# Two-layer hybrid decoder trunk on one core: later readers behind queued transposes, TensorE transposes half a step later, interleaved first loads, Strassen products for two gate projections

## The chip, the core and the metric

The kernel runs on one core of one Trainium2 chip. The metric is the device time of one execution in microseconds (us), lower is better. TensorE does the matrix products, VectorE (DVE in the profile) and ScalarE (ACT) prepare operands and finish results, GpSimd (POOL) and SyncE (SP) issue transfers; each engine works through its own queue in program order.

## The reference, cut to what matters

Two layers, 256 tokens, model width 2048, everything in float32.

```python
for l in range(DEPTH):                                   # 2
    h = rms_norm(x, mix_norm[l])
    proj = h @ w_in[l]                                   # 2048 -> q 1024 | k 256 | v 256 | u,v 2048 | gates 4096
    q, k, v, uv, gate_logits = jnp.split(proj, cuts, axis=-1)
    ...
    branch_a = sliding_window_attention(q, k, v, sinks[l]) @ w_attn_branch[l]       # 1024 -> 2048
    branch_b = chunked_sgu(jax.nn.gelu(uv), w_spatial[l], ...) @ w_sgu_branch[l]    # 1024 -> 2048
    gates = jax.nn.sigmoid(gate_logits)
    merged = gates[..., :D_MODEL] * branch_a + gates[..., D_MODEL:] * branch_b
    x = x + merged @ w_out[l]
    h2 = rms_norm(x, ffn_norm[l])
    x = x + (jax.nn.silu(h2 @ w_gate[l]) * (h2 @ w_up[l])) @ w_down[l]              # 2048 -> 5632 -> 2048
return x
```

## The kernel before

**A product in three passes.** A float32 product is made of three matmuls (`three`, L318): high part by high part, high by low, low by high. For the weights, ScalarE rounds a loaded piece to its high part (`whi`, L222) and VectorE subtracts it to get the low part (`wlo`, L230), always 128x1024 at a time, for a matrix that is used once. For the activations, a "unit" of 512 rows of the contraction holds `uh` and `ul` (transposed high and low part, L426 and L433, or L451 and L438), for all 256 tokens.

**Jobs and steps.** The work is a list of jobs (`add_job`, L106), each one 1024 (or 512) output columns of one weight matrix, run one after the other by `run` (L323). A plain job goes over its units; each unit gives four steps of 12 matmuls (two halves of the rows, two halves `c` of the columns). A step is one slot of time in the schedule (`tick`, L269). In the order of a layer the jobs are: q and k/v, v, u, gate a (columns 0 and 1024), branch a (0, 1024), then gate b 0, branch b 0, gate b 1024, branch b 1024, then w_out 0 and 1024, then three feed-forward rounds of gate, up and down jobs (blocks 0 to 3, 4 to 7, and 8 to 10). The names used below are gate-b-0, gate-b-1024 and so on; "up job of blocks 2 and 3" is the up projection of those two 512-column blocks.

**Strassen jobs.** With `m=1` (L43: w_out, gate/up and down) the first unit of a job is done by a seven-product scheme in place of eight: products 11, t1, t2, 22, t3, 21, t4 (L87) of 6 matmuls each, half a slot each. It needs sums of weight pieces (`sum` and `raw`, L214, four VectorE operations of 128x1024) and sums of activation blocks (`sums`, `sh`, `sl`, L450 to L458). Between the products, results move among PSUM banks: ScalarE copies `a` into `x` after 11 (L358), `e` into `p` after t1 and `a` into `u` after t2 (L344), `a` into `y` after t3 (L364); VectorE adds `u` and `p` back after t4 (L366, L367). Product 22 overwrites `e`, so it waits for `p`; t3 overwrites `a`, so it waits for `u`; t4 waits for `y`; the plain step that accumulates into `e` waits for L366.

**Transposes.** A new activation is transposed in one of two ways (`transposed`, L416). Gathered: VectorE transposes 32x32 blocks (`blk`, L408), then GpSimd issues 16 small transfers (`tt<-blk`, L413), and a fixed `G_WAIT` = 5 slots later ScalarE reads `tt` into `uh`, a slot later VectorE makes `ul`. On TensorE (`on_pe`, L471): eight 128x128 transposes into PSUM (`pt`), from which ScalarE makes `uh` at once and VectorE `ul` a slot later. The third block of each product's output goes through TensorE, the others are gathered.

**What sets the order.** Each engine's order is written by hand. `after(n, f)` puts work n slots later, `soon` behind the operand preparation of the next step; `fill` (L234) keeps high parts six and low parts five pieces ahead of TensorE. Results of a job's two column halves come out in its last two steps: `scaled_into`, `gated` (L948, with `merge` L960 in branch b), `upped` (L994) or the residual add (L895), all on VectorE, and two `Square` passes per block on ScalarE (`junk`, L513).

Of the kernel before, what the change touches and what calls it, by code (L numbers as in the profile page):

```python
# [14 lines left out]
P = 128  # L15
NT = 2
S = P * NT
# [31 lines left out]
def hybrid_trunk(ctx: ExitStack, tc: tile.TileContext, x, mix_norm, w_in, q_norm, k_norm, sinks,  # L49
# [84 lines left out]
    for l in range(DEPTH):  # L134
        wl = w_in[l]
        for o in (0, None)[::-1 if l == 0 else 1]:
            add_job([wl[:, o:o + CW2] if o is not None else wl[:, O_KV:O_KV + CW]])
        for o in (O_V, O_U, O_GATE, O_GATE + CW2):
            add_job([wl[:, o:o + CW2]])
        for o in (0, CW2):  # L140
            add_job([w_attn_branch[l, :, o:o + CW2]])
        for o in (0, CW2):
            add_job([wl[:, O_GATE + D + o:O_GATE + D + o + CW2]])
            add_job([w_sgu_branch[l, :, o:o + CW2]])
# [114 lines left out]
    def after(n, fn):  # L259
        steps.append((slot_no[0] + n, fn))  # L260
# [123 lines left out]
    class Unit:  # L384


        def __init__(self, sums):
            self.hi = slot([P, 4, S], F32R, "uh")
            self.lo = slot([P, 4, S], F32R, "ul")
            if sums:  # L390
                self.shi = slot([P, 4, 2, P], F32R, "sh")
                self.slo = slot([P, 4, 2, P], F32R, "sl")

        def block(self, name, k):
            if name in ("11", "21", "t4"):
# [4 lines left out]

    def flat(v):
        return v.rearrange("p a b -> p (a b)") if len(v.shape) == 3 else v.rearrange("p a b c -> p (a b c)")

    def gathered(dst, src):

        blk = slot([P, 4, 4, NT, B], name="blk")
        for t in range(NT):
            nc.vector.transpose(blk[:, :, :, t, :].rearrange("p j k c -> p k j c"),  # L408
                                src[:, t, :].rearrange("p (k j c) -> p k j c", j=4, c=B))
        ov = dst.rearrange("p k (t i c) -> p i (k t) c", t=NT, c=B)  # L410
        for i in range(4):
            for j in range(4):
                nc.gpsimd.dma_start(ov[j * B:(j + 1) * B, i],  # L413
                                  blk[i * B:(i + 1) * B, j].rearrange("p k t c -> p (k t) c"))

    def transposed(units, c, src, scale=None, cols=None, on_pe=False, sums=False, at_once=False):  # L416

        unit = Unit(sums)

        def scaled(k):  # L420
            return (scale or 1.0) if cols is None else cols[:, k:k + 1]

        def highs(k0, n, src_t):
            step = n if cols is None else 1
            for k in range(0, n, step):
                nc.scalar.activation(unit.hi[:, k0 + k:k0 + k + step, :], src_t[:, k:k + step, :], AF.Copy,  # L426
                                     scale=scaled(k0 + k))
# [9 lines left out]
        def low(hi, lo, full):  # L437
            nc.vector.tensor_tensor(out=flat(lo), in0=flat(full), in1=flat(hi.bitcast(F32)), op=ALU.subtract)  # L438

        def ready():  # L440
            units[c] = unit

        def combined(f, n):
            s4 = slot([P, 4, 2, P], name="sums")
            a11, a12, a21, a22 = (f[:, 2 * h:2 * h + 2, t * P:(t + 1) * P] for t in range(2) for h in range(2))

            def first():
                for i, (p, q, op) in enumerate(((a21, a22, ALU.add), (s4[:, 0], a11, ALU.subtract),
                                                (a11, a21, ALU.subtract), (a12, s4[:, 1], ALU.subtract))):
                    nc.vector.tensor_tensor(out=s4[:, i], in0=p, in1=q, op=op)  # L450
                nc.scalar.activation(unit.hi, f, AF.Copy)  # L451

            def second():
                low(unit.hi, unit.lo, f)
                nc.scalar.activation(unit.shi, s4, AF.Copy)

            def third():
                low(unit.shi, unit.slo, s4)  # L458
                ready()

            for i, fn in enumerate((first, second, third)):
                after(n + i, fn)

        if on_pe:
            pts = []
            for b in range(2):
                pt = ps_at.tile([P, 2, S], F32, tag="at", name=nm("pt"))
                for kk in range(2):
                    k = 2 * b + kk
                    for t in range(NT):  # L470
                        nc.tensor.transpose(pt[:, kk, t * P:(t + 1) * P], src[:, t, k * P:(k + 1) * P], ident)  # L471
# [12 lines left out]
            return  # L484

        tt = slot([P, 4, S], name="tt")
        gathered(tt, src)
        if not sums:
            after(G_WAIT, lambda: highs(0, 4, tt))
            after(G_WAIT + 1, lambda: (lows(0, 2, tt[:, 0:2]), lows(2, 2, tt[:, 2:4]), ready()))  # L490
            return

        def scale_all():
            if cols is not None or scale is not None:
                for k in range(4) if cols is not None else (None,):
                    kk = slice(0, 4) if k is None else slice(k, k + 1)
                    nc.scalar.activation(tt[:, kk], tt[:, kk], AF.Copy, scale=scaled(k))

        after(G_WAIT, scale_all)
        combined(tt, G_WAIT + 1)  # L500

    class Norm:


        def __init__(self, cols):
            self.cols = cols
            self.ss = [tiny(NCH, f"ss{t}", 2) for t in range(NT)]
            self.units = [None] * NCH

        def squares(self, c):  # L510
            for t in range(NT):
# [139 lines left out]
    class Attention:  # L651
# [62 lines left out]
        def begin(self):  # L714
            n = Q_FIRST
            for c in range(2):
                for t in range(NT):
                    for g in (2 * c, 2 * c + 1):
                        after(n, lambda t=t, g=g: self.scores(t, g))
                        n += Q_STEP  # L720
                after(n + 7, lambda c=c: transposed(self.attT, c, self.att[c]))

        def scores(self, t, g):
            nk = P * (t + 1)
# [64 lines left out]
    class Spatial:  # L789
# [61 lines left out]
        def u(self, c, ps):  # L851
            ut = slot([P, NT, CW], name="u")
            self.gelu(ps, ut)
            for b in range(2):
                after(12 + 3 * b + 6 * c, lambda b=b: self.mix(c, b, ut))
            after(19 + 6 * c, lambda: transposed(self.sguT, c, ut))

        def mix(self, c, b, ut):
            pg = ps_at.tile([P, 2, NT, P], F32, tag="at", name=nm("psg"))
# [44 lines left out]
    for l in range(DEPTH):  # L904
# [37 lines left out]
        def branch(dst, j, units, then=None):  # L942
            def done(c, ps):
# [30 lines left out]
        for i, fs in enumerate(ROUNDS):  # L974
# [14 lines left out]
            def up_done(f, ps):  # L989
# [60 lines left out]
```

## Time and profile before

| | us |
|---|---|
| median of 2 runs | 2544.26 (2544.24 to 2544.29) |
| the profiled execution, its own time | 2546.71 |
| span of its trace | 2545.0 |
| TensorE busy in the span | 2494.3 (98%) |
| VectorE busy | 1855.0 (73%) |
| ScalarE busy | 1319.9 (52%) |
| GpSimd busy | 464.6 (18%) |

The span runs from the first to the last instruction. TensorE's granted clock is 0.996 of full speed over the span. A matmul's record is longer (391 ns) than its place in the stream, since matmuls overlap in the pipeline: what counts is the distance between the starts. Idle time of an engine is given with the engine and line that ended it.

### The profile page before, as it was taken

To read this page: it belongs to the slowest core of one execution; us is meant where nothing else is said; L and a number is where in the kernel's file an instruction comes from. 1 tells how busy PE (TensorE), PEld (TensorE's weight loads), DVE (VectorE), ACT (ScalarE), POOL (GpSimd) and SP (SyncE) were. 2 spreads that over 40 slices of the span, in tenths; PEclk is the share of its full clock that TensorE was granted. 3 is DMA by queue.
4 is the path that set the end of the run, shared out by engine and by line. 5 is a ranking of instruction groups with operands and counts; after the bars stand their busy time and mean duration, and the time that the engine had idled before them with its cause. 6 is when DMAs were issued, how large, how long until landed. Compare 5 with 4: busy or idle time off the path is not lost. (4 is left out here: it accounts for less than half of the span.)

```text
span 2545.0 us, 30534 instructions
## 1 busy us (share of the span) xinstructions
PE 2494.3 (98%) x11126; PEld 2038.9 (80%) x11126; DVE 1855.0 (73%) x2135; ACT 1319.9 (52%) x1628; POOL 464.6 (18%) x767
## 2 busy tenths in 40 slices
PE   9999999999999999999999999999999999999999
PEld 7888888778788878888778888887787888788877
DVE  6796546787877687777768955468778776877686
ACT  5455444465555555455554544445655455645554
POOL 1512202140210021003225032022302100210020
PEclk9999999999999999999999999999999999999999
DMA  7745656566565657565666456665656656565654
GB/s 266 231 152 172 206 188 211 174 202 209 185 215 183 226 171 234 171 229 185 215 206 216 159 167 205 198 200 167 228 182 214 208 189 207 189 212 188 214 170 161
DMA packets 157271, 502.99 MB, mean 198 GB/s; under 512 B 19712, under 2 KB 22368, under 8 KB 157120
## 3 DMA queue, kind: packets, MB, share of 16 engines
q1 hardware_dynamic: 133408, 476.87, 56.0%
q0 software_dynamic: 23392, 23.89, 3.5%
q8 instruction: 87, 1.43, 0.2%
q14 instruction: 64, 0.52, 0.1%
q10 hardware_dynamic: 320, 0.27, 0.0%
HBM read 475.27 MB, written 2.10 MB: 188 GB/s over the span
## 5 line engine op out<-in xcount | busy, mean ns | idle before, releaser
L230 DVE TENSOR_TENSOR wlo<-raw,whi 128x1024 fp32r<-128x1024 f32 (+1 forms) x936 | 1125.9, 1221 | 513.7 <-PE acc L320 422.2
L222 ACT ACTIVATE whi<-raw 128x1024 fp32r<-128x1024 f32 (+1 forms) x936 | 972.2, 1057 | 823.0 <-PE acc L321 786.7
L319 PE MATMUL acc<-whi,uh 128*128 128x512 f32 x3204 | 1260.6, 393 | 8.0 <-DVE acc L366 3.1
L320 PE MATMUL acc<-wlo,uh 128*128 128x512 f32 x3204 | 1251.8, 391 | 4.7 <-DVE wlo L230 4.7
L321 PE MATMUL acc<-whi,ul 128*128 128x512 f32 x3204 | 1251.2, 391 | 0.0
L319 PEld LDWEIGHTS acc<-whi,uh 128*128 128x128 f32 x3204 | 603.3, 188 | 141.7 <-DVE acc L366 6.8
L320 PEld LDWEIGHTS acc<-wlo,uh 128*128 128x128 f32 x3204 | 603.5, 188 | 130.3 <-DVE wlo L230 7.4
L321 PEld LDWEIGHTS acc<-whi,ul 128*128 128x128 f32 x3204 | 603.2, 188 | 126.4
L413 POOL DMA_DIRECT2D tt<-blk x624 | 359.2, 583 | 1768.2 <-DVE blk L408 746.8
L319 PE MATMUL acc<-whi,sh 128*128 128x512 f32 x304 | 125.1, 412 | 19.9 <-ACT p L344 9.9
L222 ACT ACTIVATE whi<-sum 128x1024 fp32r<-128x1024 f32 x76 | 80.7, 1061 | 93.8 <-PE acc L321 52.0
L321 PE MATMUL acc<-whi,sl 128*128 128x512 f32 x304 | 119.2, 392 | 0.0
L320 PE MATMUL acc<-wlo,sh 128*128 128x512 f32 x304 | 119.1, 392 | 0.0
L319 PEld LDWEIGHTS acc<-whi,sh 128*128 128x128 f32 x304 | 57.3, 189 | 50.9 <-ACT p L344 19.6
L230 DVE TENSOR_TENSOR wlo<-sum,whi 128x1024 fp32r<-128x1024 f32 x76 | 92.5, 1217 | 7.1 <-PE acc L320 7.1
L433 DVE SCALAR_TENSOR_TENSOR ul<-tt,uh 128x512 fp32r<-128x512 f32 x44 | 28.4, 688 | 89.9 <-ACT uh L426 88.3
L426 ACT ACTIVATE uh<-tt 128x1024 fp32r<-128x1024 f32 x22 | 23.2, 1056 | 117.1 <-DMA tt<-blk 107.0
L321 PEld LDWEIGHTS acc<-whi,sl 128*128 128x128 f32 x304 | 57.2, 188 | 12.5
L320 PEld LDWEIGHTS acc<-wlo,sh 128*128 128x128 f32 x304 | 57.5, 189 | 9.6
L895 DVE TENSOR_TENSOR xs<-acc,xs 128x512 f32<-128x512 f32 (+1 forms) x66 | 41.4, 668 | 10.4 <-PE acc L321 10.4
L214 DVE TENSOR_TENSOR raw<-raw,sum 128x1024 f32<-128x1024 f32 x38 | 46.5, 1225 | 1.3
L214 DVE TENSOR_TENSOR sum<-raw 128x1024 f32<-128x1024 f32 x38 | 46.4, 1220 | 0.0
(140 smaller groups left out, 1119.7 us busy)
## 6 DMA issues: line engine op xcount, KB each, us to landing
raw<-in_w_in_dram SPq DMA_DIRECT2D x112, 1024.0 KB, 5.0
raw<-in_w_down_dram SPq DMA_DIRECT2D x88, 1024.0 KB, 6.0
raw<-in_w_gate_dram SPq DMA_DIRECT2D x80, 1024.0 KB, 5.5
raw<-in_w_up_dram SPq DMA_DIRECT2D x80, 1024.0 KB, 5.3
raw<-in_w_out_dram SPq DMA_DIRECT2D x32, 1024.0 KB, 6.4
tt<-blk POOLq DMA_DIRECT2D x624, 32.0 KB, 5.1
raw<-in_w_attn_branch_dram SPq DMA_DIRECT2D x16, 1024.0 KB, 5.6
raw<-in_w_sgu_branch_dram SPq DMA_DIRECT2D x16, 1024.0 KB, 5.3
```

The source lines that it names most:

```text
L214: nc.vector.tensor_tensor(out=self.raw(dst), in0=self.raw(total[0]), in1=self.raw(total[1]), op=ALU.subtract)
L222: nc.scalar.activation(hi[:, k, :], raw[:, k, :], AF.Copy)
L230: nc.vector.tensor_tensor(out=lo[:, k, :], in0=raw[:, k, :], in1=hi[:, k, :].bitcast(F32), op=ALU.subtract)
L319: nc.tensor.matmul(ps, a, hi, start=first, stop=False, skip_group_check=True)
L320: nc.tensor.matmul(ps, a, lo, start=False, stop=False, skip_group_check=True)
L321: nc.tensor.matmul(ps, b, hi, start=False, stop=last, skip_group_check=True)
L413: nc.gpsimd.dma_start(ov[j * B:(j + 1) * B, i], blk[i * B:(i + 1) * B, j].rearrange("p k t c -> p (k t) c"))
L426: nc.scalar.activation(unit.hi[:, k0 + k:k0 + k + step, :], src_t[:, k:k + step, :], AF.Copy, scale=scaled(k0 + k))
L433: nc.vector.scalar_tensor_tensor(out=flat(unit.lo[:, kk, :]), in0=flat(src_t[:, k:k + step, :]), scalar=scaled(k0 + k), in1=flat(unit.hi[: ...
L895: nc.vector.tensor_tensor(out=xs[:, t, sl], in0=ps[t][:, i * w:(i + 1) * w], in1=xs[:, t, sl], op=ALU.add)
```

## The change

Four edits, with few lines of code:

1. The reader of a gathered transpose is placed by a running end of GpSimd's queue: each gather takes 3.5 slots from the end of the one before it, and its reader comes 1.5 slots after its end. A gather by itself keeps its 5 slots; one that is asked for a slot after another gets 7.5.
2. A unit turned on TensorE is turned 2 slots after its result in place of 1. Where the next job begins with Strassen's half slots, that is two products (12 matmuls) later.
3. The first loads: a weight load follows every block of x (1, 2, 3, 4 loads after blocks 0 to 3, before 1, 1, 2, 3).
4. The two gate b jobs of each layer become Strassen jobs (`M_GATE`). Their first unit has no sums from its making, so `add_sums` rebuilds the full value from high and low part and makes them, 2 slots after gate a has ended, that is in branch a 0.

```diff
-G_WAIT = 5
+G_BUSY, G_LAND = 3.5, 1.5
-LOAD_BY = (1, 1, 2, 3)
+LOAD_BY = (1, 2, 3, 4)
+M_GATE, M_ATT, M_SGU = (0, 0, 1, 1), (0, 0), (0, 0)
...
+        for i, o in enumerate((0, CW2)):
+            add_job([wl[:, O_GATE + D + o:O_GATE + D + o + CW2]], m=M_GATE[2 + i])
...
     def gathered(dst, src):
...
+        gather_end[0] = max(gather_end[0], slot_no[0]) + G_BUSY
+        return gather_end[0] + G_LAND - slot_no[0]
...
-        gathered(tt, src)
+        n = gathered(tt, src)
         if not sums:
-            after(G_WAIT, lambda: highs(0, 4, tt))
-            after(G_WAIT + 1, lambda: (lows(0, 2, tt[:, 0:2]), lows(2, 2, tt[:, 2:4]), ready()))
+            after(n, lambda: highs(0, 4, tt))
+            after(n + 1, lambda: (lows(0, 2, tt[:, 0:2]), lows(2, 2, tt[:, 2:4]), ready()))
...
-        after(G_WAIT, scale_all)
-        combined(tt, G_WAIT + 1)
+        after(n, scale_all)
+        combine(unit, tt, n + 1, ready)
...
+        def add_sums(self, c):
+
+            f = slot([P, 4, S], name="full")
+            unit = self.units[c]
+            nc.vector.tensor_tensor(out=flat(f), in0=flat(unit.hi.bitcast(F32)), in1=flat(unit.lo.bitcast(F32)), op=ALU.add)
+            unit.more()
+            combine(unit, f, 1)
...
-                    after(1, lambda: nxt.unit(o, on_pe=o == 2, sums=sums and o == 0))
+                    after(2 if o == 2 else 1, lambda: nxt.unit(o, on_pe=o == 2, sums=sums and o == 0))
...
-                    after(1, lambda: transposed(mT, j + c, ga[j + c], scale=0.5, on_pe=j + c == 2,
+                    after(2 if j + c == 2 else 1,
+                          lambda: transposed(mT, j + c, ga[j + c], scale=0.5, on_pe=j + c == 2,
                                                 sums=M_OUT and j + c == 0))
...
         for j in (0, 2):
             gate(ga, j)
+        after(2, lambda nrm=norm: nrm.add_sums(0))
...
-                after(1, lambda: transposed(hT, f, a, on_pe=f == fs[2], sums=f in fs[:M_DOWN]))
+                after(2 if f == fs[2] else 1, lambda: transposed(hT, f, a, on_pe=f == fs[2], sums=f in fs[:M_DOWN]))
```

`combine` is the old inner function `combined` made common: four sums, then high and low part of them (and of the full value, where that is still to be made).

What stands where, at three places. In the changed kernel the line of `whi` is L223, of `wlo` L231, of `p` and `u` L345, of the copies between banks L359 and L365, of `uh` L462 (L437 with sums).

ScalarE, gate job of blocks 2 and 3 in the first feed-forward round, after its Strassen part, before (`uh_5172` is hidden block 0, `uh_5227` hidden block 1):

```order
L222 ACTIVATE whi_5346<-raw_5255 128x1024
L451 ACTIVATE uh_5172<-tt_5176 128x1024
L426 ACTIVATE uh_5227<-tt_5229 128x1024
L222 ACTIVATE whi_5368<-raw_5279 128x1024
L455 ACTIVATE sh_5174<-sums_5196 128x1024
L222 ACTIVATE whi_5390<-raw_5279 128x1024
```

and now:

```order
L223 ACTIVATE whi_5395<-raw_5304 128x1024
L437 ACTIVATE uh_5221<-tt_5225 128x1024
L223 ACTIVATE whi_5416<-raw_5328 128x1024
L442 ACTIVATE sh_5223<-sums_5245 128x1024
L223 ACTIVATE whi_5436<-raw_5328 128x1024
L462 ACTIVATE uh_5276<-tt_5278 128x1024
```

The reader of the second gather has moved behind two more weight pieces and `sh`, that is by two steps.

ScalarE, start of the first gate job of the feed-forward part of layer 0 (`junk` squares, `pt` holds normed block 2), before:

```order
L426 ACTIVATE uh_4490<-pt_4492,vcols 128x256 x2
L426 ACTIVATE uh_4490<-pt_4499,vcols 128x256 x2
L222 ACTIVATE whi_4512<-raw_4331 128x1024
L358 ACTIVATE acc_4510<-acc_4508 128x512
L222 ACTIVATE whi_4526<-sum_4406 128x1024
L344 ACTIVATE p_810_4536<-acc_4509 128x512
L513 ACTIVATE junk_4538,ss_669_3786<-xs 128x512
L513 ACTIVATE junk_4540,ss_670_3787<-xs 128x512
L222 ACTIVATE whi_4568<-raw_4372 128x1024
L344 ACTIVATE u_821_4582<-acc_4508 128x512
```

and now:

```order
L223 ACTIVATE whi_4545<-raw_4376 128x1024
L359 ACTIVATE acc_4543<-acc_4541 128x512
L223 ACTIVATE whi_4559<-sum_4455 128x1024
L345 ACTIVATE p_828_4569<-acc_4542 128x512
L462 ACTIVATE uh_4571<-pt_4573,vcols 128x256 x2
L462 ACTIVATE uh_4571<-pt_4580,vcols 128x256 x2
L533 ACTIVATE junk_4587,ss_687_3821<-xs 128x512
L533 ACTIVATE junk_4589,ss_688_3822<-xs 128x512
L223 ACTIVATE whi_4613<-raw_4417 128x1024
L345 ACTIVATE u_843_4627<-acc_4541 128x512
```

The four `uh` passes have moved from ahead of the products to between `p` and `u`.

VectorE, start of gate-b-1024 of layer 0 (`gate` rows are the two column halves of branch b 0, with their merge), before:

```order
L230 TENSOR_TENSOR wlo_3263<-raw_3122,whi_3245 128x1024
L948 SCALAR_TENSOR_TENSOR gate_3115<-gate_3115,acc_3139 128x512
L960 TENSOR_TENSOR gate_2140<-gate_2140,gate_3115 128x512
L948 SCALAR_TENSOR_TENSOR gate_3115<-gate_3115,acc_3140 128x512
L960 TENSOR_TENSOR gate_2140<-gate_2140,gate_3115 128x512
L408 STREAM_TRANSPOSE blk_3288<-gate_2140 128x4x4x32 x2
L230 TENSOR_TENSOR wlo_3314<-raw_3163,whi_3261 128x1024
```

and now:

```order
L968 SCALAR_TENSOR_TENSOR gate_3145<-gate_3145,acc_3169 128x512
L981 TENSOR_TENSOR gate_2140<-gate_2140,gate_3145 128x512
L968 SCALAR_TENSOR_TENSOR gate_3145<-gate_3145,acc_3170 128x512
L981 TENSOR_TENSOR gate_2140<-gate_2140,gate_3145 128x512
L414 STREAM_TRANSPOSE blk_3318<-gate_2140 128x4x4x32 x2
L231 TENSOR_TENSOR wlo_3344<-raw_3115,whi_3293 128x1024
L215 TENSOR_TENSOR sum_3227<-raw_3152,raw_3115 128x1024
L968 SCALAR_TENSOR_TENSOR gate_3166<-gate_3166,acc_3171 128x512
L981 TENSOR_TENSOR gate_2165<-gate_2165,gate_3166 128x512
```

The sum of weight pieces for t4 stands between the two halves' merges, and five more weight pieces' low parts and L367, L368 follow. On TensorE the program has 24 matmuls fewer (6 in each of the four gate b jobs).

More of the change, by code (lines that the diff above doesn't have):

```diff
@@ L402, in flat @@
         return v.rearrange("p a b -> p (a b)") if len(v.shape) == 3 else v.rearrange("p a b c -> p (a b c)")
+    gather_end = [0]
     def gathered(dst, src):
@@ L414, in gathered, with combine, low, first @@
                                   blk[i * B:(i + 1) * B, j].rearrange("p k t c -> p (k t) c"))
+        gather_end[0] = max(gather_end[0], slot_no[0]) + G_BUSY
+        return gather_end[0] + G_LAND - slot_no[0]
+    def combine(unit, f, n, then=None):
+        s4 = slot([P, 4, 2, P], name="sums")
+        a11, a12, a21, a22 = (f[:, 2 * h:2 * h + 2, t * P:(t + 1) * P] for t in range(2) for h in range(2))
+        def low(hi, lo, full):
+            nc.vector.tensor_tensor(out=flat(lo), in0=flat(full), in1=flat(hi.bitcast(F32)), op=ALU.subtract)
+        def first():
+            for i, (p, q, op) in enumerate(((a21, a22, ALU.add), (s4[:, 0], a11, ALU.subtract),
+                                            (a11, a21, ALU.subtract), (a12, s4[:, 1], ALU.subtract))):
+                nc.vector.tensor_tensor(out=s4[:, i], in0=p, in1=q, op=op)
+            if then is not None:
+                nc.scalar.activation(unit.hi, f, AF.Copy)
+        def second():
+            if then is not None:
+                low(unit.hi, unit.lo, f)
+            nc.scalar.activation(unit.shi, s4, AF.Copy)
+        def third():
+            low(unit.shi, unit.slo, s4)
+            if then is not None:
+                then()
+        for i, fn in enumerate((first, second, third)):
+            after(n + i, fn)
     def transposed(units, c, src, scale=None, cols=None, on_pe=False, sums=False, at_once=False):
@@ L435, in lows @@
                     in1=flat(unit.hi[:, kk, :].bitcast(F32)), op0=ALU.mult, op1=ALU.subtract)
-        def low(hi, lo, full):
-            nc.vector.tensor_tensor(out=flat(lo), in0=flat(full), in1=flat(hi.bitcast(F32)), op=ALU.subtract)
         def ready():
             units[c] = unit
[L443 to L462, printed above, removed]
         if on_pe:
@@ L720, in begin @@
                         n += Q_STEP
-                after(n + 7, lambda c=c: transposed(self.attT, c, self.att[c]))
+                after(n + 7, lambda c=c: transposed(self.attT, c, self.att[c], sums=c == 0 and sum(M_ATT)))
         def scores(self, t, g):
@@ L855, in u @@
                 after(12 + 3 * b + 6 * c, lambda b=b: self.mix(c, b, ut))
-            after(19 + 6 * c, lambda: transposed(self.sguT, c, ut))
+            after(19 + 6 * c, lambda: transposed(self.sguT, c, ut, sums=c == 0 and sum(M_SGU)))
         def mix(self, c, b, ut):
```

18 lines of the change are left out of this document (9 added, 9 removed).

## The prediction

> **What bounds the kernel now.** I began with the page's head: TensorE is busy for 98% of the span, so time is won only by fewer matmuls or by its waits.
>
> ```profile
> span 2545.0 us, 30534 instructions
> PE 2494.3 (98%) x11126; PEld 2038.9 (80%) x11126; DVE 1855.0 (73%) x2135; ACT 1319.9 (52%) x1628; POOL 464.6 (18%) x767
> ```
>
> Next the waits of TensorE (total us, times, longest); these rows are 30.1 of its 50.7 us without work.
>
> ```profile
> PE acc L319 <- ACT p L344: 9.9, 13, 0.9
> PE pt L471 <- DVE xs L895: 6.7, 6, 2.2
> PE acc L320 <- DVE wlo L230: 4.7, 6, 2.6
> PE pt L471 <- DVE hid L994: 4.5, 4, 2.0
> PE acc L319 <- ACT u L344: 4.3, 5, 1.0
> ```
>
> No wait is longer than 2.6 us, and none names a transfer: TensorE waits for ScalarE and VectorE, which are idle for a quarter to a half of the time. So I asked where these run late, with a table by stage, cut at the first matmul of jobs (stage, its length, busy us of TensorE, weight loads, VectorE, ScalarE, GpSimd, then granted clock, DMA share, GB/s).
>
> ```profile
> 287.94:310.22 22.28, 22.06 (x98) 17.95 (x96) 13.34 (x13) 12.54 (x15) 0.00 (x0) 1.00 0.62 192
> 331.98:375.50 43.52, 43.52 (x194) 36.04 (x192) 20.80 (x18) 18.85 (x19) 0.00 (x0) 1.00 0.59 193
> 397.26:441.14 43.88, 43.88 (x194) 35.89 (x192) 29.72 (x34) 21.95 (x23) 18.39 (x32) 1.00 0.64 210
> 441.14:508.97 67.83, 65.67 (x291) 53.58 (x290) 51.71 (x53) 32.43 (x35) 9.19 (x16) 1.00 0.56 181
> 508.97:603.48 94.51, 88.74 (x382) 71.57 (x380) 74.00 (x90) 57.45 (x83) 29.40 (x50) 0.98 0.60 195
> 603.48:645.84 42.36, 42.36 (x187) 34.76 (x186) 31.04 (x30) 22.17 (x24) 0.00 (x0) 1.00 0.58 199
> 689.20:777.77 88.57, 86.48 (x381) 70.28 (x380) 67.64 (x68) 46.86 (x53) 9.19 (x16) 1.00 0.60 196
> 948.33:1037.27 88.94, 86.47 (x381) 70.29 (x380) 68.28 (x68) 47.46 (x53) 9.20 (x16) 1.00 0.59 195
> 1164.45:1243.54 79.09, 75.50 (x334) 61.30 (x333) 66.70 (x87) 43.58 (x49) 20.07 (x35) 1.00 0.62 201
> 1243.54:1326.81 83.27, 78.61 (x340) 63.88 (x338) 54.68 (x72) 45.22 (x68) 28.77 (x50) 0.98 0.68 216
> 1596.42:1639.94 43.52, 43.52 (x193) 36.04 (x192) 20.80 (x18) 18.84 (x19) 0.00 (x0) 1.00 0.60 194
> 1661.70:1706.77 45.07, 44.05 (x194) 35.89 (x192) 29.72 (x34) 21.96 (x23) 18.39 (x32) 1.00 0.63 205
> 1774.60:1868.80 94.20, 88.78 (x382) 71.39 (x381) 73.99 (x90) 57.44 (x83) 29.36 (x50) 0.98 0.60 196
> 1954.52:2043.36 88.84, 86.48 (x381) 70.28 (x380) 68.08 (x68) 47.13 (x53) 9.20 (x16) 1.00 0.58 196
> 2213.90:2301.90 88.00, 86.49 (x381) 70.29 (x380) 67.24 (x67) 46.66 (x52) 9.18 (x16) 1.00 0.59 197
> 2429.08:2509.50 80.42, 75.75 (x333) 61.22 (x332) 64.62 (x68) 43.70 (x49) 18.43 (x32) 1.00 0.61 196
> ```
>
> The second row is gate-b-0, plain: 192 matmuls in 43.52 us, 0.2267 each. The sixth, the up job of blocks 0 and 1, is Strassen's: 186 matmuls in 42.36, 0.2 over 186 x 0.2267. This is my clean job. The same work on blocks 2 and 3 begins at 689.20 and is not clean. Two rows of VectorE's timeline tell why, with one of ScalarE's between the two places:
>
> ```profile
> 604.66 1.22 DVE L214 TENSOR_TENSOR sum<-raw,raw 128x1024 f32<-128x1024 f32 x1
> 692.94 1.22 DVE L214 TENSOR_TENSOR sum<-raw,raw 128x1024 f32<-128x1024 f32 x1
> 674.40 1.06 ACT L426 ACTIVATE uh<-tt 128x1024 fp32r<-128x1024 f32 x1 [10.08 <-DMA tt<-blk]
> ```
>
> The sum for t4 ends 2.40 us after the clean job's start (604.66 + 1.22 - 603.48) and 4.96 after the other's: VectorE is 2.6 late. ScalarE had stood 10.08 us before the reader of the second of two gathers, with all weight pieces queued behind it, and VectorE cannot subtract what is not rounded. 15 us later the backlog isn't worked off. So the root of many short waits is one long block of an engine that looks half idle.
>
> **The change, part by part.** The sum is made against the profiled execution's span of 2545.0 (its own time is 2546.71; the median of the runs is 2544.26); I take the difference off the median.
>
> *Gate b as Strassen jobs.* Each loses 6 matmuls, 6 x 0.2267 = 1.36 us, and adds four VectorE operations of 1.22, less one `wlo`, and two adds. Gate-b-0 follows a branch job whose results take two operations per half, the shape of the clean job, and VectorE is busy for only 20.80 of 43.52: I take 42.36, a gain of 1.16, twice, **-2.3**. `add_sums` costs VectorE 1.22 + four sums + 1.22, some 4 us, in branch a 0, where it is busy for 13.34 of 22.28; without that cover it would be 4 per layer.
>
> Gate-b-1024 is another matter: branch b's merge doubles the work on the results. The nearest row is the start of w_out 0, with the same merges:
>
> ```profile
> 462.67 0.39 PE L321 MATMUL acc<-whi,ul 128*128 128x512 f32 x1
> 464.15 0.66 PE L471 MATMUL pt<-ident,gate 128*128 128x128 f32 x4 [0.98 <-DVE gate L960]
> 460.22 1.22 DVE L230 TENSOR_TENSOR wlo<-raw,whi 128x1024 fp32r<-128x1024 f32 x1 [0.36 <-PE acc L320]
> 478.13 0.69 DVE L366 TENSOR_TENSOR acc<-acc,u 128x512 f32<-128x512 f32 x1
> ```
>
> Branch b's last matmul starts at 462.67, so w_out could begin at 462.90. VectorE works without a gap from 460.22 to the end of L366 at 478.82, 15.9 us after that point, and the plain step behind t4 needs it. TensorE alone would be there after 54 x 0.2267 = 12.2. Gate-b-1024 has two block transposes in place of the two `ul`, of like size: so 3.7 us of waits, at `p` first (t4's sum stands behind the first merges) and then at L366. 42.36 + 3.7 = 46.1 in place of 43.88 and 45.07: **+3.2**. Bounds: 0 waits (42.36, -4.2 in all) and twice as much (+10.6). I take the row.
>
> *w_out 0.* Its turned block is ready without the 0.98 wait, but VectorE's chain ends where it did, and the same matmul waits for it longer: **0**, or at best -1.0 per layer.
>
> *Later readers.* A second reader comes two steps (24 matmuls, 5.4 us) later. Half of a 10 us block goes, and what still comes behind it has two pieces less to catch up, 2 x 1.22, and `sl`, 1.22: 3.7 us, more than the 2.6 of lateness. So I expect clean jobs behind it. Up job of blocks 2 and 3 (6 and 7) with the first down job: twice 42.36, the eight turned blocks, and a new wait, since `uh` now stands between `p` and `u`:
>
> ```profile
> 734.13 1.04 PE L471 MATMUL pt<-ident,hid 128*128 128x128 f32 x8
> 734.92 0.48 PE L319 MATMUL acc<-whi,uh 128*128 128x512 f32 x1
> L426 ACT ACTIVATE uh<-pt 128x512 fp32r<-128x512 f32 x16 | 8.7, 596 | 15.3 <-PE pt L471 15.3
> ```
>
> Turning takes TensorE 0.8, the two `uh` take ScalarE 1.1 with their overlap: 0.3 of wait. With 0.1 at L366 the pair is 85.9, against 88.57, 88.94, 88.84 and 88.00: **-10.7**. The last round (gate/up of block 10, then down): 324 matmuls 73.5, 0.4, 0.8, and the wait for `p` (9.9/13 = 0.8) that the block work causes anyway: 75.5 against 79.09 and 80.42, **-8.5**; here the turning comes after product 22, when `hid` is long there. Last down job and the next q: 330 matmuls 74.8, 0.2, 0.8, and 2.7 for three waits that the squares cause at `p`, `u` and `y` and that stay, each near the longest of the rows for `p` and `u` (0.9 and 1.0): 78.5 against 83.27, **-4.8**. Branch a 0 (22.28, 22.06 busy): **-0.2**.
>
> *w_out 1024 and the first gate job.* Here `uh` is four passes and two squares stand behind it:
>
> ```profile
> 557.75 1.69 ACT L426 ACTIVATE uh<-pt,vcols 128x256 fp32r<-128x256 f32 x4 [1.97 <-PE pt L471]
> 561.50 1.05 ACT L222 ACTIVATE whi<-sum 128x1024 fp32r<-128x1024 f32 x1
> 565.10 0.59 ACT L344 ACTIVATE u<-acc 128x512 f32<-128x512 f32 x1
> 568.70 0.59 ACT L364 ACTIVATE acc<-acc 128x512 f32<-128x512 f32 x1
> ```
>
> If VectorE is on time, the sum is there 2.45 us after the start; from `whi` to the end of `u` ScalarE takes 565.69 - 561.50 = 4.2, with `uh` now inside 5.8; from there to the end of L364 3.6. So t4 starts after 11.9, where matmuls and turning alone would take 36 x 0.2267 + 0.8 = 9.0: 2.9 of new wait. The pair: twice 42.36, 0.8, 2.7 in w_out 1024 as before, 2.9: 91.1 against 94.51 and 94.20, **-6.5**. With no new wait it would be -12.3.
>
> *First loads.* The longest wait at L320, 2.6, is for `wlo` and not for a load: **0**, between -2.6 and, should x come later by as much, +2.6.
>
> The clock is in these terms. Two windows and, for contrast, one more:
>
> ```profile
> 553.83:557.23 3.40, 1.15 (x6) 0.54 (x5) 3.40 (x5) 1.06 (x1) 0.00 (x0) 1.00 0.00 0
> 557.24:560.65 3.41, 3.41 (x13) 2.93 (x12) 3.17 (x4) 2.62 (x5) 0.00 (x0) 0.50 0.19 22
> 1209.18:1212.59 3.41, 1.81 (x7) 1.05 (x6) 3.41 (x5) 1.64 (x3) 0.00 (x0) 1.00 0.00 0
> ```
>
> A wait of 2 us that leaves TensorE 1.15 busy of 3.40 is followed by half clock for 3.41, a loss of up to 1.7; the window with 1.81 busy isn't. The new waits of 2 to 3 us could do the same; where ScalarE or VectorE decides anyway, it is hidden. The Trainium skill ("TensorE: Matmul & The Clock Gate", Part 1, on the HAM clock gate) says that the clock falls to half after at least one idle window of about 3.4 us. By that rule none of these waits would cost clock, and the third rival below would lose most of its price; the trace differs, since the window before the drop held 1.15 us of work.
>
> Sum: -2.3 + 3.2 + 0 - 10.7 - 8.5 - 4.8 - 0.2 - 6.5 + 0 = -29.8; 2544.26 - 29.8 = **2514.5 us**.
>
> **The rivals.** *The blocks stay.* If the second transfer still lands so late that VectorE is as late as now, the up and down pairs gain nothing, the last rounds only their waits for `hid` (4.5), the gate pair 0.6 twice, the q job 2.2 and its clock, 3.4: with -0.2 and gate b's -2.3 + 3.2 that is -8.4, **2535.9**. For it: 10.08 is nearly twice 5.4. Against: the 3.7 us of catch-up. *VectorE has more room than I think.* Gate-b-1024 comes out clean (-7.4 against mine), and the gate pair's wait is half (-2.9): **2504**. For it: 73% busy; against: the gapless 18.6 us at w_out. *The waits move into the Strassen starts.* Ten of them get `uh` between `p` and `u`, four gate b jobs are new. If TensorE stops there long enough to be granted half clock each time, 2.3 of wait (as the longest now) and 1.7 of clock at 14 places are 56 us against 29.8: **2570**, slower than before. It decides above 2.1 us per place. Against: the granted clock is short of 1.00 in only three stages of the table (0.98), and the forecast has such waits at four places.
>
> **How the numbers follow.** My forecast 0.65, blocks stay 0.17, more room 0.12, slower 0.06. The range for 8 in 10 reaches to the second rival below and most of the way to the first above: 2503 to 2532. Over 2%, about what a measurement of this kernel can tell from no change, would be below 2493.4 or above 2595.1; the first needs nearly all waits gone, the last is beyond the slow rival: 0.02, 0.97, 0.01.
>
> **What would show it.** The reader at 674 stands for 4 to 6 us, not 10, and the up job of blocks 2 and 3 takes 42.4 without the turning. No wait of `pt` for `xs` or `hid`. Gate-b-1024 is longer than plain, 46, with waits at `p` and L366; gate-b-0 shorter, 42.4. The first gate job waits for `u` and L364, 2 to 3 us in all. I am wrong if VectorE is still late at 692, if gate-b-1024 gains, or if half clock follows in more than four places.

## The result, and the profile after

The changed kernel takes 2518.64 us (2 runs, 2517.9 to 2519.38) against 2544.26: ratio 0.9899, 95% interval 0.9857 to 0.9942. That is a gain of 1%, within the 2% to which the prediction gave 0.97. The profiled execution took 2519.38, its span is 2517.7, 27.3 less than before. Head of its page, then TensorE's waits (total us, times, longest):

```profile
span 2517.7 us, 30567 instructions
PE 2481.6 (99%) x11102; PEld 2031.9 (81%) x11102; DVE 1900.4 (75%) x2183; ACT 1344.8 (53%) x1658; POOL 465.0 (18%) x767
```

```profile
PE acc L320 <- ACT p L345: 11.0, 12, 2.1
PE acc L320 <- ACT u L345: 7.9, 7, 1.7
PE acc L320 <- DVE acc L367: 3.6, 3, 1.3
PE acc L321 <- DVE wlo L231: 3.0, 2, 2.6
PE acc L320 <- ACT acc L365: 2.9, 5, 0.6
...
PE psc L755 <- DMA kT<-blk: 1.0, 1, 1.0
```

The waits of the turned blocks (`pt`) are gone; those inside the Strassen starts (`p`, `u`) have grown by 4.7 us together, and one wait names a transfer. Stages of the table before the change, cut at the same jobs, with one more (the tenth):

```profile
287.58:309.34 21.76, 21.76 (x97) 18.02 (x96) 15.91 (x18) 11.33 (x13) 0.00 (x0) 1.00 0.60 193
331.10:373.47 42.37, 42.37 (x188) 34.75 (x186) 26.09 (x24) 23.52 (x26) 0.00 (x0) 1.00 0.67 224
395.23:441.24 46.01, 42.95 (x187) 34.60 (x186) 35.73 (x40) 27.03 (x30) 18.43 (x32) 1.00 0.74 231
441.24:509.02 67.78, 65.69 (x291) 53.52 (x290) 51.70 (x53) 32.47 (x35) 9.20 (x16) 1.00 0.55 177
509.02:600.29 91.27, 86.75 (x382) 70.26 (x380) 73.98 (x90) 57.33 (x83) 29.52 (x50) 1.00 0.63 202
686.01:772.03 86.02, 86.02 (x382) 70.34 (x380) 65.34 (x65) 45.55 (x50) 9.20 (x16) 1.00 0.62 202
942.51:1028.56 86.05, 86.04 (x381) 70.33 (x380) 65.11 (x64) 45.44 (x50) 9.20 (x16) 1.00 0.61 202
1155.69:1231.73 76.04, 75.05 (x334) 61.33 (x332) 67.04 (x87) 43.98 (x49) 20.09 (x35) 1.00 0.66 209
1231.73:1310.55 78.82, 76.60 (x340) 62.53 (x339) 54.78 (x72) 45.26 (x68) 29.29 (x50) 1.00 0.72 228
1332.31:1379.33 47.02, 45.99 (x210) 37.83 (x209) 37.43 (x45) 19.47 (x20) 31.52 (x50) 1.00 0.76 238
1645.65:1691.81 46.16, 44.06 (x188) 35.97 (x187) 35.73 (x40) 27.40 (x30) 18.43 (x32) 0.96 0.72 229
1759.59:1850.81 91.22, 86.71 (x382) 70.26 (x381) 74.06 (x90) 57.45 (x83) 29.22 (x50) 1.00 0.62 202
1936.56:2022.57 86.01, 86.01 (x382) 70.35 (x381) 65.22 (x64) 45.45 (x50) 9.20 (x16) 1.00 0.61 202
2193.06:2279.39 86.33, 86.18 (x382) 70.34 (x381) 65.30 (x64) 45.50 (x50) 9.20 (x16) 1.00 0.61 201
2406.51:2482.18 75.67, 74.90 (x333) 61.33 (x332) 64.65 (x68) 43.63 (x49) 18.48 (x32) 1.00 0.65 209
```

Read them by their second number. The pairs of up and down job (sixth, seventh, and the two before the last) are filled with matmuls from end to end. Gate-b-0 is 42.37, gate-b-1024 46.01 and 46.16. The tenth row is the v job of layer 1, which the prediction didn't speak of: 45.31 before, 47.02 now. And the two rows of the timeline on which the argument rested, ScalarE's block and VectorE's sum for t4 of the up job:

```profile
672.03 1.06 ACT L462 ACTIVATE uh<-tt 128x1024 fp32r<-128x1024 f32 x1 [6.46 <-DMA tt<-blk]
...
687.19 1.22 DVE L215 TENSOR_TENSOR sum<-raw,raw 128x1024 f32<-128x1024 f32 x1
```

The block is 6.46 and no longer 10.08, and the sum is done 687.19 + 1.22 - 686.01 = 2.40 us after its job's start, the clean job's value.

### The profile page after: what moved, and what is told of

The parts are those of the page before. It is cut to its first block, busy times and chain, and to the rows that moved or that the text cites. A ratio compares the mean times of both kernels' runs of the same rounds, so it can differ in the third digit from the quotient of the medians.

```text
span 2517.7 us, 30567 instructions
## 1 busy us (share of the span) xinstructions
PE 2481.6 (99%) x11102; PEld 2031.9 (81%) x11102; DVE 1900.4 (75%) x2183; ACT 1344.8 (53%) x1658; POOL 465.0 (18%) x767
## 5 line engine op out<-in xcount | busy, mean ns | idle before, releaser
L231 DVE TENSOR_TENSOR wlo<-raw,whi 128x1024 fp32r<-128x1024 f32 (+1 forms) x940 | 1131.7, 1219 | 489.9 <-PE acc L321 401.1
L223 ACT ACTIVATE whi<-raw 128x1024 fp32r<-128x1024 f32 (+1 forms) x940 | 978.6, 1058 | 824.2 <-PE acc L322 789.9
L320 PE MATMUL acc<-whi,uh 128*128 128x512 f32 x3164 | 1240.9, 392 | 7.9 <-DVE acc L367 3.6
L321 PE MATMUL acc<-wlo,uh 128*128 128x512 f32 x3164 | 1233.0, 390 | 3.0 <-DVE wlo L231 3.0
L322 PE MATMUL acc<-whi,ul 128*128 128x512 f32 x3164 | 1233.0, 390 | 0.0
L320 PEld LDWEIGHTS acc<-whi,uh 128*128 128x128 f32 x3164 | 594.5, 188 | 139.1 <-DVE acc L367 7.4
L321 PEld LDWEIGHTS acc<-wlo,uh 128*128 128x128 f32 x3164 | 594.8, 188 | 125.2 <-DVE wlo L231 3.9
L320 PE MATMUL acc<-whi,sh 128*128 128x512 f32 x336 | 139.2, 414 | 19.1 <-ACT p L345 11.0
L223 ACT ACTIVATE whi<-sum 128x1024 fp32r<-128x1024 f32 x84 | 89.3, 1063 | 101.8 <-PE acc L322 58.0
L321 PE MATMUL acc<-wlo,sh 128*128 128x512 f32 x336 | 132.0, 393 | 0.0
L322 PE MATMUL acc<-whi,sl 128*128 128x512 f32 x336 | 131.9, 393 | 0.0
L231 DVE TENSOR_TENSOR wlo<-sum,whi 128x1024 fp32r<-128x1024 f32 x84 | 101.8, 1212 | 8.4 <-PE acc L321 8.4
L462 ACT ACTIVATE uh<-tt 128x1024 fp32r<-128x1024 f32 x22 | 23.2, 1057 | 81.1 <-DMA tt<-blk 81.1
L215 DVE TENSOR_TENSOR raw<-raw,raw 128x1024 f32<-128x1024 f32 x42 | 51.2, 1218 | 0.0
```

What stands on the lines that cost most here:

```text
L215: nc.vector.tensor_tensor(out=self.raw(dst), in0=self.raw(total[0]), in1=self.raw(total[1]), op=ALU.subtract)
L223: nc.scalar.activation(hi[:, k, :], raw[:, k, :], AF.Copy)
L231: nc.vector.tensor_tensor(out=lo[:, k, :], in0=raw[:, k, :], in1=hi[:, k, :].bitcast(F32), op=ALU.subtract)
L320: nc.tensor.matmul(ps, a, hi, start=first, stop=False, skip_group_check=True)
L321: nc.tensor.matmul(ps, a, lo, start=False, stop=False, skip_group_check=True)
L322: nc.tensor.matmul(ps, b, hi, start=False, stop=last, skip_group_check=True)
```

## The experiments

The theory: ScalarE's block before the second reader makes VectorE late, the lateness outlives the block until the next Strassen start, and the later reader cures it. First rival: the later turning, or the loads, brought the gain. Second: the blocks cost whatever their length. The kernel before ran beside every set: medians 2546.8, 2546.76 and 2546.77 (single runs 2541.0 to 2552.94). These are some 2.5 above the 2544.26 beside the change, so kernels of different sets are compared by their ratios and by their stages. "Job" times below are distances between first matmuls, each from the one profiled execution.

### One part at a time

**The readers alone** (before, with edit 1 only):

```diff
-G_WAIT = 5
+G_BUSY, G_LAND = 3.5, 1.5
...
-        gathered(tt, src)
+        n = gathered(tt, src)
```

> The kernel before with the first edit alone: readers of gathers placed by the queue's own length. My theory (the long block of ScalarE at the second reader is the root of the short waits): nearly the whole gain, 2516 us, with the up jobs of blocks 2, 3 and 6, 7 at 42.4 plus 0.8 of turning, and almost no wait of the turned blocks for xs, since VectorE is on time without their being moved. Rival one (the later turning removes the waits): 2539 or more, with the waits of pt for xs and hid as before. Rival two (the fewer matmuls of gate b carry it): 2544.

Measured: 2515.45, ratio 0.9885 (0.9869 to 0.9902), span 2513.3. Three of its stages (w_out 1024 with the first gate job, the up job of blocks 2 and 3 with its down job, first down job of the last round):

```profile
506.20:597.03 90.83, 87.03 (x382) 70.12 (x380) 74.09 (x90) 57.31 (x83) 29.37 (x50) 1.00 0.63 203
682.74:768.73 85.99, 85.71 (x381) 70.43 (x380) 65.05 (x64) 45.26 (x50) 9.19 (x16) 1.00 0.61 202
1195.77:1228.96 33.19, 32.59 (x147) 26.68 (x146) 29.36 (x46) 18.59 (x21) 0.00 (x0) 1.00 0.57 191
```

85.99 is the whole change's 86.02. Its `pt` waits have fallen from 6.7 to 0.2 (for `xs`) and from 4.5 to 1.5 (for `hid`) with the turning where it was. So this edit alone carries the whole gain (ratio 0.9885 beside the change's 0.9899, with overlapping intervals).

**The later turning alone:**

```diff
-                after(1, lambda: transposed(hT, f, a, on_pe=f == fs[2], sums=f in fs[:M_DOWN]))
+                after(2 if f == fs[2] else 1, lambda: transposed(hT, f, a, on_pe=f == fs[2], sums=f in fs[:M_DOWN]))
...
```

> The kernel before with the second edit alone: units turned on TensorE a slot later. My theory: the waits of pt for xs and hid go, but most of them come back as waits for u and for L366, since ScalarE and VectorE are as late as before: 2536, that is about -8. Rival one (the turning carries the gain): 2524 or less.

Measured: 2539.89, ratio 0.9979 (0.9970 to 0.9989). Its waits of TensorE:

```profile
PE acc L319 <- ACT p L344: 13.9, 17, 1.5
PE acc L319 <- ACT u L344: 9.4, 7, 2.5
PE acc L319 <- DVE hid L985: 4.4, 5, 1.0
```

No `pt` wait is left, but `p` has 4.0 and `u` 5.1 more than before: with VectorE and ScalarE as late as ever, most of the wait has only moved. Its up pair stays at 89.02 (88.57 before). The turning brings 0.2% where the readers bring 1.2%, so the first rival falls as far as the turning goes.

**The loads alone:**

```diff
-LOAD_BY = (1, 1, 2, 3)
+LOAD_BY = (1, 2, 3, 4)
```

> The kernel before with the third edit alone: loads of x and weights by turns. My theory: nothing, 2544.3 within 0.5, since the longest wait at the start is for wlo behind the ul of block 1 on VectorE and not for a load. Rival: that wait of 2.6 goes, 2541.7.

Measured: 2547.1, ratio 1.0002 (0.9992 to 1.0011): nothing, and the first rival falls for the loads too.

**Gate b alone** (`M_GATE`, `add_sums`; readers, turning and loads as before):

> The kernel before with the fourth edit alone: Strassen units for the gate b jobs, with the sums made in branch a 0. My theory: gate-b-0 1.15 us shorter, gate-b-1024 about 46.0 in place of 43.9 and 45.1, in all +0.9, 2545.2. Rival two (24 matmuls fewer carry a gain): -5.4, 2538.8.

```diff
+M_GATE, M_ATT, M_SGU = (0, 0, 1, 1), (0, 0), (0, 0)
...
+        after(2, lambda nrm=norm: nrm.add_sums(0))
```

Measured: 2546.14, ratio 1.0002 (0.9993 to 1.0011). Gate-b-0 and gate-b-1024 of layer 0:

```profile
329.11:371.48 42.37, 42.37 (x188) 34.76 (x187) 26.09 (x24) 23.51 (x26) 0.00 (x0) 1.00 0.67 224
393.23:439.25 46.02, 42.95 (x187) 34.61 (x186) 35.38 (x40) 26.83 (x30) 18.43 (x32) 1.00 0.68 223
```

One gains 1.15, the other loses 2.14 (0.97 in layer 1), jobs as forecast, too small together for the runs to tell from nothing.

### Why gate-b-1024 loses

**Gate-b-1024 plain again** (the change otherwise):

```diff
-M_GATE, M_ATT, M_SGU = (0, 0, 1, 1), (0, 0), (0, 0)
+M_GATE, M_ATT, M_SGU = (0, 0, 1, 0), (0, 0), (0, 0)
```

> The changed kernel with gate-b-1024 plain again (Strassen for gate-b-0 alone). My theory (VectorE's merges make that place cost more than 6 matmuls save): gate-b-1024 43.6 in place of 46.1, -5 in all, ratio to before 0.988. Rival (six matmuls fewer gain wherever they are): +2.7, ratio 0.991.

Measured: 2513.32, ratio 0.9871 (0.9854 to 0.9887); the job is 43.73 in both layers. Beside that, the Strassen form (46.01 and 46.16) costs 2.3 and 2.4 per job, more than the difference to the kernel before shows. The 45.07 that layer 1 had before held a wait of 1.02 for `wlo` that does not return: with the loads alone, where this job's code is the same, it takes 43.77.

**No merge in branch b** (Strassen in both gate b jobs):

```diff
-            branch(gb, j, spa.sguT, merge)
+            branch(gb, j, spa.sguT, lambda j, t: None)
```

> The changed kernel without the merge: the gated branch b is not added to branch a, four VectorE adds of 0.69 fewer behind each branch b job. My theory (VectorE's chain of merges sets the waits at the start of gate-b-1024 and w_out 0): both fall by 2.7, from 46.0 to about 43.3, four places, with the wait for p down from 2.1 to under 0.5. Rival (ScalarE's copies or the granted clock set them): both stay at 46.

Measured in a single run: 2507.52, span 2505.8. Gate-b-1024:

```profile
393.40:436.60 43.20, 42.55 (x187) 34.76 (x186) 32.56 (x36) 26.69 (x30) 18.45 (x32) 1.00 0.77 246
```

46.01 has become 43.20, and w_out 0, whose start has the same merges, goes from 46.02 to 43.53. The wait for `p` in gate-b-1024 falls from 2.10 to 0.65, and that for L367 is gone. So two VectorE operations per column half were most of the price of the Strassen form here: 2.8 of the 3.6 us over a clean job's 42.4. What the merges cost by their own time, and what by the transposes that wait for them, this run does not tell apart.

### What is left in the starts

**Squares later** (gate-b-1024 plain; the two `Square` passes three slots later, on ScalarE behind `u` and `y`):

```diff
-                    after(2, lambda: nxt.squares(o))
+                    after(5, lambda: nxt.squares(o))
...
-                        after(4, lambda: nxt.finish())
+                        after(7, lambda: nxt.finish())
```

> e5 with the squares for the next norm three slots later, out of Strassen's products, and the norm's end three slots later with them. My theory (ScalarE's queue between p, u and y sets these waits): w_out 1024 and the last down job lose the waits for u and y, 1.9 each in three jobs, the first gate jobs 2.3 each: -10 against e5, ratio 0.984. Rival (VectorE's chain, or a transfer, sets them): no change.

Measured: 2507.37, ratio 0.9846 (0.9832 to 0.9861), 6.0 less than the kernel without this edit. Its w_out 1024 and last down job of layer 0, 45.28 and 34.40 in the changed kernel:

```profile
506.69:549.88 43.19, 42.54 (x187) 34.76 (x186) 36.12 (x41) 28.38 (x41) 18.48 (x32) 1.00 0.70 219
1226.74:1259.06 32.32, 31.67 (x139) 25.74 (x138) 24.57 (x31) 21.28 (x34) 18.50 (x32) 1.00 0.82 261
```

Each start with squares gets rid of some 2.1 us of waits, and the first gate jobs are 1.6 shorter (46.91 to 45.29, 45.99 to 44.41; the granted clock over the first of these was 0.96 and is 1.00 now). The q job of layer 1 gives 1.26 of it back (44.42 to 45.68), with a wait of 0.97 for `xs`.

**TensorE's transposes four slots after the result**, on top of it:

```diff
-                    after(2 if o == 2 else 1, lambda: nxt.unit(o, on_pe=o == 2, sums=sums and o == 0))
+                    after(4 if o == 2 else 1, lambda: nxt.unit(o, on_pe=o == 2, sums=sums and o == 0))
...
```

> e7 with the units of the norms and of the hidden blocks turned on TensorE two slots later still, behind product 21 in place of t1, so that uh stands behind the copies p, u and y. My theory: first gate jobs 0.6 and first down jobs 0.4 shorter each, -3 against e7, ratio 0.983. Rival (the place of uh does not matter): same as e7.

Measured: 2505.83, ratio 0.9841 (0.9827 to 0.9856), 1.5 less; this is no more than the runs scatter (2505.05 to 2506.33 beside 2503.96 to 2509.31), so the stages must show it. The first gate jobs are 44.50 and 43.81, by 0.8 and 0.6 shorter; but the v job of layer 1 takes 48.59, with 0.96 of the clock. Its row, and two stretches at the scores:

```profile
1323.38:1371.97 48.59, 47.59 (x210) 38.96 (x209) 37.71 (x46) 19.48 (x20) 31.36 (x50) 0.96 0.75 233
...
1364.50:1367.90 3.40, 2.40 (x14) 1.68 (x13) 2.73 (x4) 1.83 (x3) 0.00 (x0) 1.00 0.51 148
1368.30:1371.70 3.40, 3.40 (x9) 2.63 (x8) 2.32 (x6) 0.69 (x1) 0.00 (x0) 0.50 0.71 278
```

Half clock follows here on a stretch with 2.40 us of work, more than the 1.81 after which the prediction saw none. So the busy time before it does not by itself decide whether the clock falls.

### How short must a block be?

**Readers two slots later still** (the change with `G_LAND` 3.5):

> The change with every reader of a gather two slots later still (landing 3.5 slots in place of 1.5; nothing else). In the changed kernel ScalarE still stands 118 us before such readers, up to 6.7 at a time. Theory (a block costs only if VectorE is still behind at the next Strassen start, and it no longer is): the blocks shrink from 118 to some 30 us, and the time stays that of the change, 2518.6, give or take 1.5. Rival (each us of block costs, whatever follows: the first 50 us less brought some 25): another 25 to 40 us, 2480 to 2495. Third: the readers come so late that they fall among the next job's copies or its own unit is late: 2522 or more, with waits for p, u or the unit.

```diff
-G_BUSY, G_LAND = 3.5, 1.5
+G_BUSY, G_LAND = 3.5, 3.5
```

Measured: 2518.28, ratio 0.9887 (0.9871 to 0.9902). ScalarE's total wait at these readers and, from its timeline, the two rows of the up job that starts at 684.40:

```profile
ACT uh L462 <- DMA tt<-blk: 9.4, 10, 2.3
```

```profile
671.66 1.06 ACT L462 ACTIVATE uh<-tt 128x1024 fp32r<-128x1024 f32 x1 [2.25 <-DMA tt<-blk]
...
685.59 1.22 DVE L215 TENSOR_TENSOR sum<-raw,raw 128x1024 f32<-128x1024 f32 x1
```

The same line of the changed kernel reads 99.8 us. 90 us less of blocking bought nothing: the sum ends 2.41 after its start, as with 6.46. The second rival falls.

**Half way** (the second reader one step later in place of two):

```diff
-G_BUSY, G_LAND = 3.5, 1.5
+G_BUSY, G_LAND = 2.25, 2.75
```

> The change with its gathers given 2.25 slots of queue and 2.75 of landing in place of 3.5 and 1.5: the reader of a gather by itself stands where it was (5 slots), that of a second gather asked for a slot later comes one step later than before the change in place of two. Theory of a lag that is worked off (VectorE was 2.6 us late at the up job's sum; one step, 12 matmuls, is 2.7 us, and one piece less stands behind the block): one step is enough, the up job of blocks 2 and 3 keeps 42.6 to 43.2, the pairs 86 to 86.5, and the time is that of the change within 2 us, 2517 to 2521. Rival (the gain goes in proportion to the block): half of the gain of the pairs and rounds is lost: pairs 87.3, time 2528 to 2533.

Measured: 2522.99, ratio 0.9904 (0.9885 to 0.9922): between the two ranges. The up jobs that start at 686.52 and 946.51, block and sum of each:

```profile
674.87 1.06 ACT L462 ACTIVATE uh<-tt 128x1024 fp32r<-128x1024 f32 x1 [8.79 <-DMA tt<-blk]
...
691.16 1.22 DVE L215 TENSOR_TENSOR sum<-raw,raw 128x1024 f32<-128x1024 f32 x1
...
931.89 1.06 ACT L462 ACTIVATE uh<-tt 128x1024 fp32r<-128x1024 f32 x1 [7.33 <-DMA tt<-blk]
...
948.18 1.22 DVE L215 TENSOR_TENSOR sum<-raw,raw 128x1024 f32<-128x1024 f32 x1
```

The sums end 5.86 and 2.89 after the start, and the jobs take 45.81 and 42.88. In the other two places, with blocks of 6.98 and 7.40, they end 2.40 and 2.64 after it, and the jobs take 42.39 and 42.92. The place with 8.79 lay so far above since its transfer came later: its reader starts 11.65 before the job, the others 14.62 to 15.28. It makes up 3.4 of the 6.6 us by which this profiled execution (span 2524.3) is longer than the changed kernel's. The first gate jobs are longer by 2.1 together, the first down jobs of the last rounds by 2.3; the start and the v job of layer 1 are shorter.

The length of a block does not settle what it costs: with the loads alone one of 8.65 left the sum 5.23 after its start, and in the kernel before one of 9.60 left it 4.39. What repeats is the work behind the block. From the start of the blocked reader to the end of the sum it is 19.76 to 19.78 us in all sixteen places of the four kernels with the old placing (the kernel before, and turning, loads and gate b alone), 17.51 in the three late places here, and 16.35 in the one place with the changed kernel's order that is late (transposes four slots later: a block of 6.18, the sum at 2.50); behind the reader VectorE has no pause in any of these. So a later reader takes work away from behind the block. A sum at 2.40 needs the reader to start that much less 2.40 before the up job, 17.4 us before the change, 15.1 half way and 13.9 in the changed kernel's order, and it is late by what is missing there.

### The scores and the late transfer

**Scores two slots later** (the kernel with squares and transposes later still):

```diff
-Q_FIRST = 15
+Q_FIRST = 17
```

> The kernel with plain gate-b-1024, later squares and TensorE transposes four slots after the result (2505.83, span 2503.1), and the attention scores two slots later (17 in place of 15), 24 matmuls or 5.4 us behind. Theory (the scores waited for the gather of kT, whose last piece landed 1 to 3 us late, and the half clock behind it was that wait's): the wait goes in layer 1, the v job falls from 48.6 to 45.5, span 2500, time 2503, ratio to before 0.983. Rival (scores later make the attention's own chain late): branch a's first unit or its transposes come late, and what v gains shows up before branch a 0 as a new wait: 2506 or more.

Measured: 2503.14, ratio 0.9828 (0.9813 to 0.9843), the lowest median of all, though the interval overlaps that of the kernel without this edit. Its v job of layer 1:

```profile
1323.47:1367.92 44.45, 44.45 (x201) 36.87 (x200) 34.92 (x41) 19.41 (x20) 31.50 (x50) 1.00 0.76 232
```

48.59 has become 44.45. Some of this is work of the scores that now stands in the jobs behind it: from the v job's start to branch a 0 of layer 1 it is 207.30 without this edit and 203.94 with it, 3.4 us won, with no new wait. In layer 0 it is 203.98 and 203.94.

## Why the prediction was right, and where its sizes were off

The forecast was 2514.5 (2503 to 2532), the result 2518.64, the sum -29.8, the span's difference -27.3. Terms, forecast and measured as differences of the stages:

| term | forecast | measured |
|---|---|---|
| gate-b-0 | -2.3 | -2.30 |
| gate-b-1024 | +3.2 | +3.22 |
| w_out 0 and the branch job ahead of it | 0 | -0.10 |
| up pairs | -10.7 | -9.95 |
| last rounds | -8.5 | -7.80 |
| last down job and q | -4.8 | -4.45 |
| branch a 0 | -0.2 | -0.52 |
| w_out 1024 and first gate job | -6.5 | -6.22 |
| start, first loads | 0 | -0.41 |
| v and u of layer 1 | not named | +1.36 |

**The step that carried it**, "So I expect clean jobs behind it", is shown by the readers alone, by the sum's 2.40 us, and by the half-way kernel. The prediction set 3.7 us of catch-up against 2.6 of lateness; measured, the work from the reader to the end of the sum is 3.4 us shorter (19.76 to 16.35): behind the reader there are two `wlo` and the `sl` fewer on VectorE, just the three that were named. What it had not seen is how little is left over: the four readers of the changed kernel start 13.98 to 14.60 us before their up jobs, where 13.9 are needed. The block at the first place is 6.46, a little over the 4 to 6 that the prediction named as a sign.

**The later turning** brings nothing to the pairs on top of the readers: with them alone the pair is 85.99. Elsewhere the change and the readers alone differ: the down jobs of the last rounds are 1.8 and 1.1 shorter in the change, the first gate jobs 1.2 longer each. No run has the readers and the turning without the rest. The readers alone (2515.45), and the change without gate-b-1024's Strassen form (2513.32), are both a little under the whole change's 2518.64; the intervals of their ratios overlap with its own.

**Gate-b-1024** was the term taken from the row of w_out 0, and the job's length is right: 46.1 forecast, 46.01 and 46.16 measured. That the difference also comes out at 3.2 owes 1.3 us to chance, the long 45.07 of the one execution before; beside the plain job of 43.73 the form costs 4.7 in both layers. Its main cause is shown by the kernel without merges. The waits stand where they were put, `p` and L367 (L366 before), as the first two rows show; the others belong to the next two paragraphs:

```profile
401.57 0.50 PE L320 MATMUL acc<-whi,sh 128*128 128x512 f32 x1 [2.10 <-ACT p L345]
...
411.19 0.50 PE L320 MATMUL acc<-whi,uh 128*128 128x512 f32 x1 [0.96 <-DVE acc L367]
...
562.51 0.50 PE L320 MATMUL acc<-whi,sh 128*128 128x512 f32 x1 [1.71 <-ACT u L345]
...
566.11 0.50 PE L320 MATMUL acc<-whi,uh 128*128 128x512 f32 x1 [0.57 <-ACT acc L365]
...
1375.87 0.68 PE L755 MATMUL psc<-kT,qT 64*128 64x128 f32 x4 [1.03 <-DMA kT<-blk]
```

The first gate job waits 1.71 + 0.57 = 2.3 for `u` and L365 where 2.9 were forecast: ScalarE's queue, shown by the two kernels that moved squares and turned blocks out of it.

**What was mis-sized**: the up pairs, the last rounds and the q job by 1.8 together (0.1 to 0.5 per stage: waits of tenths that were costed as clean), and a term that was not in the sum, the last row of the fence above: the scores of layer 1 waited 1.03 for the gather of kT, and the v and u jobs took 1.36 more together. The sum of the table is -27.2. The rest of the 4.1 us between 2514.5 and 2518.64 lies in the runs: the profiled execution of before was 2.45 over the median of its runs, that of the change 0.74.

**The rivals.** "The blocks stay" was wrong on the catch-up; the half-way kernel's late place, 45.81, shows what it would have looked like. "More room" is refuted by 46.01. For "the waits move into the Strassen starts" the waits did move, `p` and `u` by 4.7 us, but none of them was longer than 2.1, and half clock followed in one window behind a Strassen start:

```profile
1649.13:1652.54 3.41, 1.31 (x6) 0.78 (x5) 3.34 (x6) 2.15 (x3) 3.41 (x7) 1.00 0.43 79
1652.54:1655.95 3.41, 3.41 (x9) 2.64 (x8) 3.41 (x5) 2.83 (x4) 2.94 (x6) 0.50 1.02 346
```

It lies in gate-b-1024 of layer 1, where VectorE decides anyway (46.16 beside 46.01 in layer 0). The Trainium skill ("TensorE: Matmul & The Clock Gate", Part 1, on the HAM clock gate) asks for a whole idle window before the drop; this one had 1.31 us of work in 3.41, so the trace differs from it once more. The three such windows of before have gone. Part of this is luck: the same first gate job took 46.97 and 47.03 in the half-way kernel, with 0.96 of the clock, and 45.99 and 45.94 in the change, with 1.00; with gate-b-1024 plain it took 46.91 at 0.96 in one layer and 45.99 at 1.00 in the other. So this rival's price is real at such a start, some 1.0 us, but it is not paid each time.

## What to carry to other kernels

An in-order engine that looks half idle can still set the time, through one long block before a late transfer: look for the idle time just before the reader, and for how late the next engine still is at the next start that needs it. What counts there is when the block ends and how much work stands behind it in the queue, not how long it was. Placing the reader by the end of the queue that feeds it is worth as much as the lateness that outlives the block, and nothing beyond. And a form with fewer matmuls pays only where the engine that must prepare it has room in that same place: the identical edit gained 1.15 us behind one job and lost 2.1 behind another.

## What the runs showed of the hardware that was not expected

- The start varies by itself. The first job (k/v) took 32.41 us before, 31.41 in the changed kernel, 29.86 with the readers alone, 31.33 with later squares and 29.82 with later transposes, though the first and third of these have the same code there, and the last two as well; the granted clock over it was 0.89 in the changed kernel and 0.94 with the readers alone. So 2.7 us of difference in this job between two executions say nothing of an edit.
- The 16 issues of kT's gather in layer 1 stop in their midst. In the changed kernel GpSimd stood 4.30 us before the tenth (1.23 was the longest such pause before the change), and the scores waited:

```profile
1357.94 5.17 POOL L419 DMA_DIRECT2D kT<-blk  x9
1367.41 4.02 POOL L419 DMA_DIRECT2D kT<-blk  x7 [4.30 <-issue]
```

  Over all kernels the wait goes by when the last of the 16 is issued. Up to 37.2 us after the v job's start there was none (the kernel before, readers, loads and gate b alone, without the merge, the two other placings of the readers). From 37.7 on, with the scores where they were, there was one of 0.4 to 1.7 (the later turning alone, the change, gate-b-1024 plain, later squares, later transposes). The pause is only one way to be late: in the last three of these no two issues are more than 2.0 apart, but the gather begins at 26.5 to 26.9, where the changed kernel begins at 25.6. What makes the pause is open; scores two slots later take the price away.
